# Moving the tile grid of a GELU-gated product by half a tile, with GELU in place

## The chip, the core and the metric

The kernel runs on one core of one Trainium2 chip. The metric is the device time in microseconds (us). Three runs of the kernel before gave 469.43, 469.44 and 469.3, so the median is 469.43 us.

The core has several engines that run at the same time. Three of them matter here: ScalarE (ACT in the profile) computes GELU, VectorE (DVE) multiplies, and SyncE (SP) only issues transfers. ScalarE issues transfers as well. A transfer issued from SP goes to one DMA queue (q1 in the profile), one issued from ScalarE to another (q10), and the same 16 DMA engines serve both queues. An instruction that has to wait for a semaphore holds up everything behind it on its own engine.

## The reference

```python
batch, seq, dim = (32, 512, 2048)          # float32
x1, x2 = x[..., :1024], x[..., 1024:]
gelu_x1 = 0.5 * x1 * (1 + erf(x1 / np.sqrt(2)))
return (gelu_x1 * x2).astype(np.float32)
```

Flattened, x is 16,384 rows of 2,048 numbers (134.2 MB), and the output is 16,384 rows of 1,024 numbers (67.1 MB).

## The kernel before

The rows are cut into 16 tiles. A tile has 128 partitions with R = 8 consecutive rows in each, so a partition of a tile is one run of 64 KB in x and one run of 32 KB in the output. A load of a tile moves 8.4 MB, a store 4.2 MB. There are two input buffers (x0_tile, x1_tile) and two output buffers (o0_tile, o1_tile); tile i uses number i % 2 of each.

The order of the work is written out by hand with semaphores; no scheduler changes it. For each tile i, in steps of some rows (5 and 3 for an ordinary tile; 2, 2 and 4 for the first and the last):

- ScalarE (line 87) reads the left half of the rows from the input buffer and writes GELU of it into the output buffer. Ahead of the first step it waits for `ready[k]`. This semaphore counts both the load of tile i and the store of tile i-2, so ScalarE starts a tile when its input has landed and the output buffer is free.
- VectorE (line 95) waits for that GELU and multiplies the output buffer in place by the right half of the input buffer.
- Behind the last step, SP waits for the products of tile i and issues the load of tile i+2 (line 115, the transfer itself on line 49), and ScalarE waits for the same products and issues the store of tile i (lines 112 and 56). The stores of the last two tiles are issued by SP.

The first tile is loaded in two halves of four rows, each with a semaphore of its own (`first`), and stored in two halves of four rows. The last tile is stored in two halves too. A small transfer into a scrap tile (line 63) opens ScalarE's queue at the start. At the end the semaphores are cleared, and SP waits for `tail_stored`, which counts the three stores that SP issued.

Of the kernel before, what the change touches and what calls it, by code (L numbers as in the profile page):

```python
# [1 line left out]

# [4 lines left out]

GELU = mybir.ActivationFunctionType.Gelu


@with_exitstack
def kernel(
    ctx: ExitStack,
    tc: tile.TileContext,
    x: bass.AP,
    out: bass.AP,
):
    nc = tc.nc
    P = nc.NUM_PARTITIONS

    x_flat = x.flatten_outer_dims()
    out_flat = out.flatten_outer_dims()
    n_rows, dim = x_flat.shape
    half = dim // 2

    R = 8
    x_t = x_flat.rearrange("(n p r) d -> n p r d", p=P, r=R)
    o_t = out_flat.rearrange("(n p r) d -> n p r d", p=P, r=R)
    n_tiles = x_t.shape[0]
    x_bufs = [nc.alloc_sbuf_tensor(f"x{k}_tile", [P, R, dim], x.dtype) for k in range(2)]  # L30
    o_bufs = [nc.alloc_sbuf_tensor(f"o{k}_tile", [P, R, half], out.dtype) for k in range(2)]

    first = [nc.alloc_semaphore(f"first{j}") for j in range(2)]
    ready = [nc.alloc_semaphore(f"ready{k}") for k in range(2)]
    gelu_done = nc.alloc_semaphore("gelu_done")
    mul_done = nc.alloc_semaphore("mul_done")
    tail_stored = nc.alloc_semaphore("tail_stored")
    opened = nc.alloc_semaphore("opened")  # L40
    scrap = nc.alloc_sbuf_tensor("scrap_tile", [8, 128], x.dtype)
    n = {sem.name: 0 for sem in [*first, *ready, gelu_done, mul_done, tail_stored, opened]}

    def counted(ins, sem, by):
        ins.then_inc(sem, by)
        n[sem.name] += by

    def load(i, rows, sem):
        ins = nc.sync.dma_start(out=x_bufs[i % 2][:, rows, :], in_=x_t[i][:, rows, :])  # L49
        counted(ins, sem, 16)  # L50
        return ins

    def store(queue, i, rows, sem):
        queue.wait_ge(mul_done, n[mul_done.name])
        counted(
            queue.dma_start(out=o_t[i][:, rows, :], in_=o_bufs[i % 2][:, rows, :]), sem, 16
        )

    opening = nc.scalar.dma_start(out=scrap[:, :], in_=x_t[0][:8, 0, :128])
    counted(opening, opened, 16)
    for ins in (
        opening,
        load(0, slice(0, 4), first[0]),
        load(0, slice(4, 8), first[1]),
        load(1, slice(0, 8), ready[1]),
    ):  # L70
        tc.no_tile_sem_insts.add(ins.ins.name)
    tc.close()
    tc.compile()  # L73

    for i in range(n_tiles):
        k = i % 2
        last = i == n_tiles - 1
        pieces = i == 0 or last
        steps = ((0, 2), (2, 4), (4, 8)) if pieces else ((0, 5), (5, 8))
        for lo, hi in steps:  # L80
            rows = slice(lo, hi)
            if i == 0 and lo % 4 == 0:
                nc.scalar.wait_ge(first[lo // 4], 16)
            elif lo == 0:
                nc.scalar.wait_ge(ready[k], n[ready[k].name])
            counted(
                nc.scalar.activation(  # L87
                    out=o_bufs[k][:, rows, :], in_=x_bufs[k][:, rows, :half], func=GELU
                ),
                gelu_done,  # L90
                1,
            )
            nc.vector.wait_ge(gelu_done, n[gelu_done.name])
            counted(
                nc.vector.tensor_mul(  # L95
                    out=o_bufs[k][:, rows, :],
                    in0=o_bufs[k][:, rows, :],
                    in1=x_bufs[k][:, rows, half:],
                ),
                mul_done,  # L100
                1,
            )
            if pieces and hi % 4 == 0:
                if last:
                    store(nc.sync, i, slice(hi - 4, hi), tail_stored)
                else:
                    store(nc.scalar, i, slice(hi - 4, hi), ready[k])
        if not pieces:
            if i == n_tiles - 2:
                store(nc.sync, i, slice(0, R), tail_stored)  # L110
            else:
                store(nc.scalar, i, slice(0, R), ready[k])
        if i + 2 < n_tiles:
            nc.sync.wait_ge(mul_done, n[mul_done.name])
            load(i + 2, slice(0, R), ready[k])


    nc.scalar.wait_ge(opened, 16)
    nc.scalar.drain()  # L119
    for sem in (*first, *ready, opened):  # L120
        nc.scalar.sem_clear(sem)
    nc.vector.drain()
    nc.vector.sem_clear(gelu_done)
    nc.sync.sem_clear(mul_done)
    nc.sync.wait_ge(tail_stored, n[tail_stored.name]).then_inc(
        tail_stored, -n[tail_stored.name]
    )


# [1 line left out]
_INS = ['x']  # L131
_OUTS = [((32, 512, 1024), 'float32')]


# [23 lines left out]
```

## Time and profile before

| what | value |
|---|---|
| runs | 469.43, 469.44, 469.3 us; median 469.43 us |
| span of the profiled execution, first to last instruction | 467.8 us |
| time outside the span, median less span | 1.6 us |
| VectorE busy | 140.5 us, 30% of the span, 34 products |
| ScalarE busy | 115.5 us, 25% of the span, 34 GELUs and a table load |
| moved by DMA | 201.34 MB, mean 430 GB/s |
| GELU of 5, 4, 3, 2 rows | 4.469, 3.608, 2.747, 1.901 us |
| product of 5, 4, 3, 2 rows | 5.493, 4.424, 3.351, 2.288 us |
| load of a full tile, issue to landing | median 44.4 us |
| store of a full tile from ScalarE, issue to landing | median 44.7 us |

The profiled execution gives its span; the time outside it, 1.6 us, is the difference from the median and is taken as the same for both kernels. A busy time is the time in which the engine worked. The DMA figures come from records of single packets; a packet here is one run of one partition, and one transfer of a 128-partition tile gives 8 packets to each of the 16 DMA engines. The shares of the queues are shares of the 16 engines' time together. Each transfer also has 16 packets of a few bytes, which signal its semaphore.

### The profile page before, as it was taken

How to read it: one execution, taken by the hardware profiler on the slowest of the kernel's cores; microseconds unless marked ns; L12 is line 12 of the kernel's file. 1: busy time of each engine (PE TensorE's matmuls, PEld its weight loads, DVE VectorE, ACT ScalarE, POOL GpSimd, SP SyncE). 2: the span in 40 equal slices, each digit the busy share in tenths (PEclk: the TensorE clock that was granted, in tenths of full speed). 3: DMA queues.
4: the chain of work that ended last, by engine and by line, in shares of the span. 5: the costliest groups of instructions: out<-in, count | busy, mean ns of one | idle time of the engine just before them, and what ended most of it. 6: DMA issues, size and time to landing. Idle time of an engine off the chain costs nothing.

```text
span 467.8 us, 154 instructions
## 1 busy us (share of the span) xinstructions
DVE 140.5 (30%) x34; ACT 115.5 (25%) x35; POOL 0.2 (0%) x4
## 2 busy tenths in 40 slices
DVE  0330515207051060511606115060150702507043
ACT  1320606041060410604105050050501506014060
POOL 0000000000000000000000000000000000000000
DMA  8999999999999999999999999999999999999988
GB/s 359 448 448 448 398 406 496 403 403 448 459 437 403 440 412 493 403 403 448 487 409 403 445 406 493 403 403 448 493 403 403 448 426 471 403 426 426 493 384 379
DMA packets 5057, 201.34 MB, mean 430 GB/s; under 512 B 568, under 2 KB 576, under 8 KB 576
## 3 DMA queue, kind: packets, MB, share of 16 engines
q1 hardware_dynamic: 2880, 142.61, 70.6%
q10 hardware_dynamic: 2176, 58.73, 29.1%
q14 instruction: 1, 0.01, 0.0%
HBM read 134.22 MB, written 67.11 MB: 430 GB/s over the span
## 4 chain that ended last, share of the span: by engine, by line
DMA 76%; DVE 14%; ACT 8%; ACTq 0%; SPq 0%; issue 0%
DMA out_dram<-o_tile 66%; DVE o_tile L95 14%; DMA x_tile<-in_x_dram 10%; ACT o_tile L87 8%; ACTq L119 0%; SPq L49 0%
## 5 line engine op out<-in xcount | busy, mean ns | idle before, releaser
L95 DVE TENSOR_TENSOR o_tile<-o_tile,x_tile 128x5120 f32<-128x5120 f32 (+3 forms) x34 | 140.5, 4171 | 319.7 <-ACT o_tile L87 319.7
L87 ACT ACTIVATE o_tile<-x_tile 128x5120 f32<-128x5120 f32 (+3 forms) x34 | 114.3, 3407 | 337.3 <-DMA out_dram<-o_tile 301.8
L87 ACT ACT_TABLE_LOAD x1 | 1.3, 1283 | 2.9 <-PEq L73 2.9
L142 POOL MEMSET const-bfloat16-1.0<- 128x1 bf16 x1 | 0.1, 102 | 0.0
L142 POOL MEMSET const-uint8-127<- 128x1 uint8 x1 | 0.1, 101 | 0.0
L142 POOL MEMSET const-float32-0.0<- 128x1 f32 x1 | 0.1, 99 | 0.2 <-issue 0.2
L142 POOL MEMSET const-float32-1.0<- 128x1 f32 x1 | 0.1, 98 | 0.0
## 6 DMA issues: line engine op xcount, KB each, us to landing
out_dram<-o_tile ACTq DMA_DIRECT2D x13, 4096.0 KB, 44.7
x_tile<-in_x_dram SPq DMA_DIRECT2D x2, 4096.0 KB, 16.7
out_dram<-o_tile ACTq DMA_DIRECT2D x2, 2048.0 KB, 34.4
out_dram<-o_tile SPq DMA_DIRECT2D x1, 4096.0 KB, 25.2
out_dram<-o_tile SPq DMA_DIRECT2D x2, 2048.0 KB, 7.8
x_tile<-in_x_dram SPq DMA_DIRECT2D x15, 44.4
scrap_tile<-in_x_dram ACTq DMA_DIRECT2D x1, 4.0 KB
```

Source lines behind the costliest of these rows:

```text
L87: nc.scalar.activation(out=o_bufs[k][:, rows, :], in_=x_bufs[k][:, rows, :half], func=GELU),
L95: nc.vector.tensor_mul(out=o_bufs[k][:, rows, :], in0=o_bufs[k][:, rows, :], in1=x_bufs[k][:, rows, half:],),
L142: nc = _bacc.Bacc("TRN2", target_bir_lowering=False, num_devices=1)
```

## The change

The grid of tiles is moved by half a tile. There are now 17 tiles: the first and the last have four rows a partition, the fifteen between have eight. The first tile is one load of four rows, and the second, of eight rows, is queued right behind it. The first tile is stored in two pieces of two rows; the last is stored whole.

GELU is written back over the left half of the input buffer, and the product goes from the input buffer to the output buffer. ScalarE therefore no longer waits for the store of tile i-2 ahead of GELU: the semaphore `ready` is split into `loaded`, for which ScalarE waits, and `stored`, for which VectorE waits ahead of the first product of a tile. The last tile's product is written into the input buffer of the tile before it, so that it waits for no store. The number of products and GELUs stays 34 each, the number of stores 18; the number of loads goes from 18 to 17.

```diff
-    R = 8
-    x_t = x_flat.rearrange("(n p r) d -> n p r d", p=P, r=R)
-    o_t = out_flat.rearrange("(n p r) d -> n p r d", p=P, r=R)
-    n_tiles = x_t.shape[0]
+    R, EDGE = 8, 4
+    bounds = [0, EDGE * P, *range((EDGE + R) * P, n_rows, R * P), n_rows]
+    n_tiles = len(bounds) - 1
+    depth = [(bounds[i + 1] - bounds[i]) // P for i in range(n_tiles)]
...
-    first = [nc.alloc_semaphore(f"first{j}") for j in range(2)]
-    ready = [nc.alloc_semaphore(f"ready{k}") for k in range(2)]
+    loaded = [nc.alloc_semaphore(f"loaded{k}") for k in range(2)]
+    stored = [nc.alloc_semaphore(f"stored{k}") for k in range(2)]
...
+    def out_tile(i):
+        if i == n_tiles - 1:
+            flat = x_bufs[(i - 1) % 2].rearrange("p r d -> p (r d)")
+            return flat[:, : R * half].rearrange("p (r d) -> p r d", r=R)
+        return o_bufs[i % 2]
...
-        pieces = i == 0 or last
-        steps = ((0, 2), (2, 4), (4, 8)) if pieces else ((0, 5), (5, 8))
+        steps = ((0, 2), (2, 4)) if depth[i] == EDGE else ((0, 5), (5, 8))
+        products_before = n[mul_done.name]
         for lo, hi in steps:
-            rows = slice(lo, hi)
-            if i == 0 and lo % 4 == 0:
-                nc.scalar.wait_ge(first[lo // 4], 16)
-            elif lo == 0:
-                nc.scalar.wait_ge(ready[k], n[ready[k].name])
-            counted(
-                nc.scalar.activation(
-                    out=o_bufs[k][:, rows, :], in_=x_bufs[k][:, rows, :half], func=GELU
-                ),
-                gelu_done,
-                1,
-            )
+            if lo == 0:
+                nc.scalar.wait_ge(loaded[k], n[loaded[k].name])
+            gelu = x_bufs[k][:, lo:hi, :half]
+            counted(nc.scalar.activation(out=gelu, in_=gelu, func=GELU), gelu_done, 1)
             nc.vector.wait_ge(gelu_done, n[gelu_done.name])
+            if lo == 0 and last:
+                nc.vector.wait_ge(mul_done, products_before)
+            elif lo == 0 and n[stored[k].name]:
+                nc.vector.wait_ge(stored[k], n[stored[k].name])
             counted(
                 nc.vector.tensor_mul(
-                    out=o_bufs[k][:, rows, :],
-                    in0=o_bufs[k][:, rows, :],
-                    in1=x_bufs[k][:, rows, half:],
+                    out=out_tile(i)[:, lo:hi, :], in0=gelu, in1=x_bufs[k][:, lo:hi, half:]
                 ),
                 mul_done,
                 1,
             )
-            if pieces and hi % 4 == 0:
-                if last:
-                    store(nc.sync, i, slice(hi - 4, hi), tail_stored)
-                else:
-                    store(nc.scalar, i, slice(hi - 4, hi), ready[k])
-        if not pieces:
-            if i == n_tiles - 2:
-                store(nc.sync, i, slice(0, R), tail_stored)
-            else:
-                store(nc.scalar, i, slice(0, R), ready[k])
+            if i == 0:
+                store(nc.scalar, i, lo, hi, stored[k])
         if i + 2 < n_tiles:
             nc.sync.wait_ge(mul_done, n[mul_done.name])
-            load(i + 2, slice(0, R), ready[k])
+            load(i + 2)
+        if i >= n_tiles - 2:
+            store(nc.sync, i, 0, depth[i], tail_stored)
+        elif i > 0:
+            store(nc.scalar, i, 0, R, tail_stored if i == n_tiles - 3 else stored[k])
```

More of the change, by code (lines that the diff above doesn't have):

```diff
@@ L24, with tile_of @@
     half = dim // 2
-    R = 8
-    x_t = x_flat.rearrange("(n p r) d -> n p r d", p=P, r=R)
-    o_t = out_flat.rearrange("(n p r) d -> n p r d", p=P, r=R)
-    n_tiles = x_t.shape[0]
+    R, EDGE = 8, 4
+    bounds = [0, EDGE * P, *range((EDGE + R) * P, n_rows, R * P), n_rows]
+    n_tiles = len(bounds) - 1
+    depth = [(bounds[i + 1] - bounds[i]) // P for i in range(n_tiles)]
+    def tile_of(flat, i):
+        return flat[bounds[i] : bounds[i + 1], :].rearrange("(p r) d -> p r d", p=P)
     x_bufs = [nc.alloc_sbuf_tensor(f"x{k}_tile", [P, R, dim], x.dtype) for k in range(2)]
     o_bufs = [nc.alloc_sbuf_tensor(f"o{k}_tile", [P, R, half], out.dtype) for k in range(2)]
-    first = [nc.alloc_semaphore(f"first{j}") for j in range(2)]
-    ready = [nc.alloc_semaphore(f"ready{k}") for k in range(2)]
+    loaded = [nc.alloc_semaphore(f"loaded{k}") for k in range(2)]
+    stored = [nc.alloc_semaphore(f"stored{k}") for k in range(2)]
     gelu_done = nc.alloc_semaphore("gelu_done")
@@ L41 @@
     scrap = nc.alloc_sbuf_tensor("scrap_tile", [8, 128], x.dtype)
-    n = {sem.name: 0 for sem in [*first, *ready, gelu_done, mul_done, tail_stored, opened]}
+    n = {
+        sem.name: 0
+        for sem in [*loaded, *stored, gelu_done, mul_done, tail_stored, opened]
+    }
     def counted(ins, sem, by):
@@ L46, in counted, with load, store @@
         n[sem.name] += by
-    def load(i, rows, sem):
-        ins = nc.sync.dma_start(out=x_bufs[i % 2][:, rows, :], in_=x_t[i][:, rows, :])
-        counted(ins, sem, 16)
+    def out_tile(i):
[3 more added lines that the diff above has]
+        return o_bufs[i % 2]
+    def load(i):
+        ins = nc.sync.dma_start(out=x_bufs[i % 2][:, : depth[i], :], in_=tile_of(x_flat, i))
+        counted(ins, loaded[i % 2], 16)
         return ins
-    def store(queue, i, rows, sem):
+    def store(queue, i, lo, hi, sem):
         queue.wait_ge(mul_done, n[mul_done.name])
         counted(
-            queue.dma_start(out=o_t[i][:, rows, :], in_=o_bufs[i % 2][:, rows, :]), sem, 16
+            queue.dma_start(out=tile_of(out_flat, i)[:, lo:hi, :], in_=out_tile(i)[:, lo:hi, :]),
+            sem,
+            16,
         )
-    opening = nc.scalar.dma_start(out=scrap[:, :], in_=x_t[0][:8, 0, :128])
+    opening = nc.scalar.dma_start(out=scrap[:, :], in_=x_flat[:8, :128])
     counted(opening, opened, 16)
[L65 to L70, printed above, removed]
+    for ins in (opening, load(0), load(1)):
         tc.no_tile_sem_insts.add(ins.ins.name)
@@ L102 @@
             )
-            if pieces and hi % 4 == 0:
-                if last:
-                    store(nc.sync, i, slice(hi - 4, hi), tail_stored)
-                else:
-                    store(nc.scalar, i, slice(hi - 4, hi), ready[k])
-        if not pieces:
-            if i == n_tiles - 2:
-                store(nc.sync, i, slice(0, R), tail_stored)
-            else:
-                store(nc.scalar, i, slice(0, R), ready[k])
+            if i == 0:
+                store(nc.scalar, i, lo, hi, stored[k])
         if i + 2 < n_tiles:
             nc.sync.wait_ge(mul_done, n[mul_done.name])
-            load(i + 2, slice(0, R), ready[k])
+            load(i + 2)
[3 more added lines that the diff above has]
+            store(nc.scalar, i, 0, R, tail_stored if i == n_tiles - 3 else stored[k])
     nc.scalar.wait_ge(opened, 16)
     nc.scalar.drain()
-    for sem in (*first, *ready, opened):
+    nc.scalar.sem_clear(opened)
+    for sem in loaded:
         nc.scalar.sem_clear(sem)
     nc.vector.drain()
-    nc.vector.sem_clear(gelu_done)
+    for sem in (gelu_done, *stored):
+        nc.vector.sem_clear(sem)
     nc.sync.sem_clear(mul_done)
```

## The prediction

> **What bounds the kernel now.** I read the page first. Both compute engines are idle for most of the span, and the row of the DMA engines is full.
>
> ```profile
> span 467.8 us, 154 instructions
> DVE 140.5 (30%) x34; ACT 115.5 (25%) x35; POOL 0.2 (0%) x4
> q1 hardware_dynamic: 2880, 142.61, 70.6%
> q10 hardware_dynamic: 2176, 58.73, 29.1%
> DMA 76%; DVE 14%; ACT 8%; ACTq 0%; SPq 0%; issue 0%
> ```
>
> The queue shares add up to 99.7% of 16 engines' span. The fifth line, the chain that ended last, puts 22% on DVE and ACT, which suggests exposed compute; so I ask the waits next.
>
> ```profile
> ACT o_tile L87 <- DMA out_dram<-o_tile: 301.8, 14, 21.9
> ```
>
> ScalarE waited 301.8 us for stores in 14 waits. That is the wait the change takes from it. Whether it cost time depends on what the DMA engines did meanwhile, so the third view is the table by windows (length, DVE, ACT, POOL, clock, DMA share, GB/s):
>
> ```profile
> 1.70:467.40 465.70, 140.48 (x34) 115.54 (x35) 0.00 (x0) 1.00 1.00 432
> 129.40:419.40 290.00, 87.61 (x20) 71.23 (x20) 0.00 (x0) 1.00 1.00 434
> ```
>
> From 1.7 to 467.4 us the 16 DMA engines are busy at share 1.00, and over ten tiles in the middle they move 434 GB/s. While one tile is computed, the transfers of the other fill the engines. The chain follows waits, but the time is set by bytes: all 201 MB go through engines that never pause.
>
> Last I read the DMA view in three windows: ten middle tiles (129.4 to 419.4), 30 to 42, and 460.2 to 461.2 (packets, MB, share):
>
> ```profile
> q1 hardware_dynamic: 1440, 83.89, 66.7%
> q10 hardware_dynamic: 1440, 41.94, 33.5%
> ...
> q1 hardware_dynamic: 64, 4.19, 81.4%
> q10 hardware_dynamic: 64, 1.05, 20.4%
> ...
> q14 instruction: 1, 0.01, 1.9%
> ```
>
> They show two things. The queues alternate packet by packet, 64 against 64, even where a store packet (16 KB) is a quarter of a load packet (64 KB). And they price packets. In the first window each queue has 1280 data packets and 160 signals: a load packet takes 66.7% x 16 x 290 / 1280 = 2.418 us, a 32 KB store packet 33.5% gives 1.214. In the second, 16 KB takes 20.4% x 16 x 12 / 64 = 0.612. In the third, one 8 KB packet (of instructions) takes 1.9% x 16 x 1 = 0.304. Time goes with bytes.
>
> **The change, part by part.** *Packets.* Full loads stay 15 and half loads 2. Full stores go from 14 to 15, 16 KB stores from 4 to 1, and two 8 KB stores are new. A transfer is 8 packets an engine, so an engine's load work stays 120 x 2.418 + 16 x 1.213 = 309.6 us, and its store work goes from 112 x 1.213 + 32 x 0.612 = 155.4 to 120 x 1.213 + 8 x 0.612 + 16 x 0.304 = 155.3. The total is 465.0 before and 464.9 after: -0.1 us. The 8 KB price is the one unknown: no store packet of that size is in the trace. Bounds are half of 16 KB (0.304 agrees) and no saving at all against 16 KB (0.612), so 0 to +4.9 us; I take the lower, as 64, 32 and 16 KB are proportional within 1.5%.
>
> *The load removed.* One DMA issue fewer (0.42 us on SP at 1.16 in the chain, ahead of nothing but load 1): nothing. The first packet waits for the first issue, at 0.73, as before.
>
> *Start.* Load 0 lands as before, and GELU starts at 12.79. On ScalarE the first store now stands between the two GELUs and waits for the first product, so the sequence is 1.90 + 2.29, a store at about 17.0, 0.36 of issue, 1.90 + 2.29, a store at 21.6. SP issues load 2 then, not at 30.6. Queue q1 still has load 1 (8 x 2.418 = 19 us from about 11.1), so the engines are covered. Store packets begin after some 12 load packets (8 of load 0, 4 of load 1), at 20.8: an estimate from the first store before, which was issued at 19.26 and still had no packet in the window 20.5 to 24.2, so 1.0 us (first issue to first packet at 0.73 to 1.7) to 5.2 us of lag.
>
> *Middle.* From there one load packet goes with one store packet. Tile 0's stores are 16 small packets an engine, not 8, so the stores run 8 packets more behind the loads: load i (1 to 15) ends at load packet 8 + 8i, store i at store packet 16 + 8i, that is at load packet 28 + 8i. The product of tile i waits for store i-2 (load packet 12 + 8i), four packets after load i has ended. Then it takes 5.49 + 3.35 = 8.84, and load i+2 is issued. Load i+1 has four packets left at the wait's end, 4 x (2.418 + 1.213) = 14.5 us, against 0.4 (landing: last packet at 467.4, span's end at 467.8) + 8.84 + 1.0 to 5.2 = 10.2 to 14.4. So q1 just does not run dry. If it does, q10 still holds a whole store and the engines go on. Behind VectorE's waiting product nothing else stands; behind its result stand SP's load and ScalarE's store, and behind that store the next GELU. So ScalarE still stops at store i-2, by way of the product. In the trace this costs nothing while a queue holds packets; without that cover a period would show its 13.3 us of compute, 4.47 + 8.84.
>
> *GELU in place, other addresses, three semaphore clears more on VectorE's and ScalarE's queues*: the same row counts at the same prices on engines 70% and 75% idle; the clears run under the last stores. Nothing.
>
> *End.* Store 13 ends at load packet 132, four into load 16's eight. From that point E the queues hold 4 load and 8 store packets of 32 KB, 12 x 1.213 = 14.6 us. Store 15's first packet comes 10.2 to 14.4 after E: no gap. Load 16 has landed by E + 10.1, GELU and product of 2 + 2 rows end by E + 16.7, and store 16 is queued there, while stores 14 and 15 hold the engines until 14.6 + 8 x 1.213 = 24.3. Then 8 x 0.612, and the end at E + 29.2, with no pause in the engines. The end before is as tight: share 0.94 in its last 7.2 us, so about 0.3 us is to be had.
>
> Sum: 467.8 - 0.1 for packets, 0 to -0.3 at the end, 0 elsewhere. I take 467.8, and with 1.6 outside the span 469.4 us.
>
> **Rivals.** *Faster: a fixed cost of each transfer is on the path, and one load fewer saves it.* For it: one issue disappears, and a store's wait leaves ScalarE. Against it: the engines are busy from 1.7 to 467.4, so all that is not packets is 1.7 + 0.4 + (465.7 - 465.0) = 2.8 us, and the first packet's 1.7 and the landing's 0.4 stay. The most that it could give is 0.7, or 468.7. To pass 0.2% (0.94 us, about what a measurement here can tell from no change) it needs faster packets too: about 468.3. Chance 0.04.
> The Trainium skill, "DMA: Bandwidth & Descriptors", section "Anatomy of one DMA", charges each DMA some 2.0 us of setup and completion besides its bytes; a load fewer would then be an estimated 2.0 us, 467.4. The trace disagrees for queued transfers: 434 GB/s across twenty of them leaves no room for it.
>
> *Slower: the small stores cost by the packet.* If an 8 KB packet takes what 16 KB takes, 16 x (0.612 - 0.304) = 4.9 us come on top: 474.3. It decides from 0.304 + 0.94 / 16 = 0.36 us a packet on. For it: no 8 KB store has run here. Against: the 0.304 row and the proportion. Chance 0.04.
> The Trainium skill, "DMA: Bandwidth & Descriptors", section "Bandwidth", gives 6.15 us for 1 MB (measured there on transfers issued from GpSimd); tile 0's stores are just that size, and at 2.42 us by this trace's 434 GB/s each would lose an estimated 3.7 us, 476.9 for two. In the window 30 to 42, with small stores beside a load, the trace shows 437 GB/s together, which speaks against it.
>
> *Slower: a gap at the end.* If store packets begin one load packet later, or a store lands more slowly than 0.4, the cover after E is 13.3 instead of 14.6 against up to 14.4, and both queues are empty for up to 1.1 us: 470.5. It decides from 14.6 us between E and store 15's first packet. For it: store 15 comes from a product that now waits for a store. Against: the lag must be at its upper bound. Chance 0.07.
>
> *The wait only changes its owner.* ScalarE stops at its own store instruction, which waits for the product, which waits for the older store. I hold this to be so in the middle, and it gives the same time as the forecast, 469.4.
>
> **Numbers.** The forecast holds with 0.85: engines full before and after, the same bytes. Faster 0.04, slower 0.04 + 0.07 = 0.11. The range goes from 469.0, the 0.3 at the end and 0.1 for packets, to 470.3, most of the gap.
>
> **What would show it.** Right: DMA share 1.00 from 1.7 to the end, 434 GB/s in the middle, first stores landing near 62 us, ScalarE's waits for stores gone from the list and about as long on loads, VectorE waiting for stores. The 8 KB stores' packets should have a share that gives 0.30 us each. Wrong: a window with a share below 0.9, above all between 440 and 460, or a load packet longer than 2.42 beside 8 KB ones.

## The result and the profile after

The changed kernel takes 470.08 us (median of 19 runs) where the kernel before takes 469.30 (19 runs). The ratio is 1.0017 with a 95% interval of 1.0010 to 1.0023. So it is slower by 0.8 us: less than the 0.94 us that the prediction took for the limit of what can be told from no change, but the interval of these runs does not hold 1. The direction "no change" was wrong, by a small amount.

The page of the changed kernel, its busy times, queues and chain:

```profile
span 468.2 us, 169 instructions
DVE 140.5 (30%) x34; ACT 115.6 (25%) x35; POOL 0.2 (0%) x4
q1 hardware_dynamic: 2736, 140.51, 69.6%
q10 hardware_dynamic: 2320, 60.82, 30.1%
DMA 81%; DVE 15%; ACT 1%; DVEq 1%; issue 0%; ACTq 0%
```

Its list of waits (who waited for what: us in total, times, longest):

```profile
ACT x_tile L88 <- DMA x_tile<-in_x_dram: 332.8, 17, 22.1
DVE o_tile L95 <- DMA out_dram<-o_tile: 276.8, 14, 20.7
```

The change did what it says. ScalarE's 301.8 us of waits for stores are gone; it waits 332.8 us for loads, and VectorE has the 276.8 us of waits for stores. The chain that ended last now has 1% of ScalarE in place of 8%.

The table by windows (length, DVE, ACT, POOL, clock, DMA share, GB/s) shows the DMA engines as full as before:

```profile
1.70:467.40 465.70, 140.48 (x34) 115.64 (x35) 0.00 (x0) 1.00 1.00 432
129.40:419.40 290.00, 87.61 (x21) 71.22 (x20) 0.00 (x0) 1.00 1.00 434
```

The middle moves the same 434 GB/s. The 0.8 us are therefore neither in the middle nor in idle DMA engines. Two places remain: the time outside the span, and transfers that run but take too long.

**Outside the span.** Every run has its time and its span. In 35 runs of the kernel before, the median span is 468.0 and the time outside 1.33 us; in the changed kernel's 19 runs they are 468.5 and 1.62. So 0.3 us of the 0.8 lie outside the span and 0.5 inside. (The execution that the prediction used, 467.8, was one of the shortest of the kernel before; hence its 1.6 outside.) The changed execution of the page, 468.2, is one of the shortest of its 19 too.

**Inside the span.** The DMA view by windows prices single load packets: the window holds the start of one packet on each of the 16 engines, so share x window x 16 / packets is the mean time of one. At 60.4 to 61.4, and at 62.9 to 63.9 (packets, MB, share):

```profile
q1 hardware_dynamic: 16, 1.05, 241.8%
q10 hardware_dynamic: 16, 0.13, 30.9%
...
q1 hardware_dynamic: 16, 1.05, 294.8%
q10 hardware_dynamic: 16, 0.00, 0.9%
```

In the first window a 64 KB load packet takes 2.418 us, its usual time, and an 8 KB store packet 0.309. In the second, 2.5 us later, the same kind of load packet takes 2.948 us on all 16 engines. In it q10 has only the 16 signals of tile 0's second store: this is the load packet between the last 8 KB store packet and the first 32 KB one. A smaller one is at 30.1 to 30.8 (2.50 us), in the middle of tile 0's first store.

The kernel before has such a place as well, from 21.6 to 22.2, ahead of its first store packet at 24.4. The view counts 16 signals of 0.009 us with the 16 load packets, so a load packet there takes 445.6% x 16 x 0.6 / 16 less 0.009, or 2.66 us:

```profile
q1 hardware_dynamic: 32, 1.05, 445.6%
```

I went through the packet records of each trace in this way: for every data packet, its time less the usual one for its size (2.418, 1.213, 0.611 or 0.309 us), summed from 12 to 100 us and divided by 16 engines. The kernel before has 0.41 us of such excess, the changed kernel 0.68. After 100 us both have 0.02 or 0.03. Ahead of 12 us, where the first load packets run, the two pages have 0.60 and 0.76.

### The profile page after: what moved, and what is told of

It is laid out like the page before. It is cut to its first block, busy times and chain, and to the rows that moved or that the text cites. A ratio compares the mean times of both kernels' runs of the same rounds, so it can differ in the third digit from the quotient of the medians.

```text
span 468.2 us, 169 instructions
## 1 busy us (share of the span) xinstructions
DVE 140.5 (30%) x34; ACT 115.6 (25%) x35; POOL 0.2 (0%) x4
## 3 DMA queue, kind: packets, MB, share of 16 engines
q10 hardware_dynamic: 2320, 60.82, 30.1%
## 4 chain that ended last, share of the span: by engine, by line
DMA 81%; DVE 15%; ACT 1%; DVEq 1%; issue 0%; ACTq 0%
DMA out_dram<-o_tile 72%; DVE o_tile L95 14%; DMA x_tile<-in_x_dram 9%; ACT x_tile L88 1%; DVE x_tile L95 0%; DVEq L116 0%; ACTq L67 0%; DVEq L93 0%
## 5 line engine op out<-in xcount | busy, mean ns | idle before, releaser
L95 DVE TENSOR_TENSOR o_tile<-x_tile 128x5120 f32<-128x5120 f32 (+2 forms) x32 | 136.0, 4288 | 310.6 <-DMA out_dram<-o_tile 276.8
L88 ACT ACTIVATE x_tile<-x_tile 128x5120 f32<-128x5120 f32 (+2 forms) x34 | 114.4, 3407 | 335.6 <-DMA x_tile<-in_x_dram 332.8
L95 DVE TENSOR_TENSOR x_tile<-x_tile 128x2048 f32<-128x2048 f32 x2 | 4.5, 2288 | 5.3 <-ACT x_tile L88 5.3
```

The costliest lines, as they stand in the source:

```text
L88: counted(nc.scalar.activation(out=gelu, in_=gelu, func=GELU), gelu_done, 1)
L95: nc.vector.tensor_mul(out=out_tile(i)[:, lo:hi, :], in0=gelu, in1=x_bufs[k][:, lo:hi, half:]),
```

## The experiments

Times and ratios are against the kernel before on the same chip, whose median was 469.24 to 469.32 us in every group.

### Once more, as a yardstick, and three parts of the change

I began with three theories: A, the 8 KB stores and the long load packets behind them at 63 us; B, the moved waits and GELU in place; C, the end of the moved grid.

> The changed kernel once more, as the yardstick of this group and for a second trace. All theories: 469.9 to 470.3 us, ratio 1.0015 to 1.0020 to the kernel before. Theory A (the long load packets around 63 us, where ScalarE's queue goes over from 8 KB to 32 KB store packets, are the cost): they are there again, 16 of them, 0.4 us or more too long each. Theory B (waits) and theory C (the end) need no long packets at 63 us; if they are gone here and the time is still 470, theory A is wrong.

Measured: 470.17 us, ratio 1.0018 (1.0010 to 1.0027), span 468.5, outside 1.62. The excess was 0.76 us, at the same places (30, 52 and 63 us), but spread otherwise: 0.30 at 30 us and only 0.14 at 63. So theory A's "0.4 us each at 63 us" was too narrow; the sum repeats, the places share it differently.

Tile 0 stored whole:

```diff
-            if i == 0:
-                store(nc.scalar, i, lo, hi, stored[k])
...
-        elif i > 0:
-            store(nc.scalar, i, 0, R, tail_stored if i == n_tiles - 3 else stored[k])
+        else:
+            store(nc.scalar, i, 0, depth[i], tail_stored if i == n_tiles - 3 else stored[k])
```

> The changed kernel, but tile 0 is stored whole, with 16 KB packets, behind its second product; everything else as changed. Theory A: the 8 KB packets and the long load packets at 63 us go, 469.3 to 469.5. Theory B (VectorE's wait, GELU in place) and theory C (the end of the grid: a queue for each of the last two stores): 470.1 as changed.

Measured: 469.97 us, ratio 1.0019 (1.0011 to 1.0027). Theory A falls: without any 8 KB packet the time stays. The excess stays too, 0.78 us, now mostly in one load packet an engine at 31 us.

The grid alone:

```diff
-            gelu = x_bufs[k][:, lo:hi, :half]
-            counted(nc.scalar.activation(out=gelu, in_=gelu, func=GELU), gelu_done, 1)
+                if not last and n[stored[k].name]:
+                    nc.scalar.wait_ge(stored[k], n[stored[k].name])
+            raw = x_bufs[k][:, lo:hi, :half]
+            gelu = raw if last else out_tile(i)[:, lo:hi, :]
+            counted(nc.scalar.activation(out=gelu, in_=raw, func=GELU), gelu_done, 1)
...
-            elif lo == 0 and n[stored[k].name]:
-                nc.vector.wait_ge(stored[k], n[stored[k].name])
...
```

> The grid alone: 17 tiles and the stores of the changed kernel, but GELU goes to the output buffer and ScalarE waits for both the load and the store, as before; only the last tile is done in place. Theory A and theory C: 470.1 as changed. Theory B: back to 469.3.

Measured: 470.38 us, ratio 1.0022 (1.0014 to 1.0031), but made up differently: span 469.1, outside 1.31. The long packets at the start are there (0.80 us). Another 0.6 us comes at the end: here SP's queue had run empty before store 15 was issued at 451.8, and the first packets of that store, which start while ScalarE's queue still runs store 14, took up to 1 us too long. The DMA view from 452.6 to 453.6 shows it, 15 packets of 32 KB at 171.4% x 16 / 15 = 1.83 us, not 1.21:

```profile
q1 hardware_dynamic: 15, 0.49, 171.4%
```

The waits alone:

```diff
-                    out=o_bufs[k][:, rows, :], in_=x_bufs[k][:, rows, :half], func=GELU
+                    out=x_bufs[k][:, rows, :half], in_=x_bufs[k][:, rows, :half], func=GELU
...
             nc.vector.wait_ge(gelu_done, n[gelu_done.name])
+            if lo == 0 and n[stored[k].name]:
+                nc.vector.wait_ge(stored[k], n[stored[k].name])
...
-                    in0=o_bufs[k][:, rows, :],
+                    in0=x_bufs[k][:, rows, :half],
...
```

> The waits alone: 16 tiles, loads and stores of the kernel before, but GELU in place in the input buffer and VectorE waiting for stores. Theory A and theory C: 469.3 as before. Theory B: 470.1.

Measured: 469.59 us, ratio 1.0004 (0.9996 to 1.0013), span 468.1, outside 1.48. The interval holds 1, so the total decides little. What is plain is that the span hardly moves, while the time outside grows by 0.15.

These four split the question. The span's 0.5 us goes with the grid, the time outside with the waits and what was moved with them (1.31 where ScalarE waits for stores, 1.5 to 1.6 where VectorE does).

### The time outside the span

The semaphores that count stores are cleared at the end by the engine that waits for them. In the changed kernel VectorE clears three, before it cleared one. Here SP clears the two:

```diff
-    for sem in (gelu_done, *stored):
-        nc.vector.sem_clear(sem)
-    nc.sync.sem_clear(mul_done)
+    nc.vector.sem_clear(gelu_done)
+    for sem in (mul_done, *stored):
+        nc.sync.sem_clear(sem)
```

> The changed kernel, but the two semaphores that count stores are cleared by SP at the end, not by VectorE; VectorE clears one semaphore as before. So far the time outside the span is 1.3 us in the three kernels in which ScalarE waits for stores and 1.5 to 1.6 us in those in which VectorE waits. If VectorE's two added clears cost this: 1.3 outside, 469.8 in all. If it is VectorE's added waits (17 more instructions in its program) or anything else: 1.6 outside, 470.1. The span stays at 468.5 by all theories.

Measured: 469.73 us, ratio 1.0012 (1.0003 to 1.0021), span 468.4, outside 1.34 (1.31 to 1.37 in 11 runs). The 0.28 us are gone. They came from VectorE's two added clears, although in the trace these end at 456.6, some 12 us before the span does. VectorE's added waits, which are all still there, cost nothing outside. Nor do the two clears on ScalarE, where the kernel with the grid alone has them (1.31). The price is not a fixed one: the kernel with the waits alone has the same two clears more on VectorE, and there the time outside grew by 0.15.

Taking the last clear from VectorE in the kernel before as well would then make that kernel faster, if the price were per clear:

```diff
-    nc.vector.sem_clear(gelu_done)
-    nc.sync.sem_clear(mul_done)
+    for sem in (mul_done, gelu_done):
+        nc.sync.sem_clear(sem)
```

> The kernel before, but the one semaphore that VectorE clears at the end is cleared by SP too. If each clear on VectorE costs 0.14 us outside the span (0.28 for two), the time outside falls from 1.33 to 1.2 and the time to 469.15. If only more than one clear costs, nothing changes: 469.3.

Measured: 469.19 us, ratio 1.0000 (0.9991 to 1.0009), outside 1.32. It is no price per clear: the first costs nothing. What takes the time outside the span was not seen, as no record lies there.

### The start or the end of the grid

Theory A had failed, and of theory B only the time outside was left, which came from the clears. For the span I put three others: S, load packets of 64 KB that run from 12 us on beside the first stores; E, the end of the grid; R, a queue that is slow when it is used first.

Tile 1 loaded in two halves, so that the order of loads at the start is nearer to that before (the deciding line):

```diff
...
+        pieces = ((0, 4), (4, 8)) if i == 1 else ((0, depth[i]),)
...
```

> The changed kernel, but tile 1 is loaded in two halves of four rows (32 KB packets), so that 64 KB packets begin after the third half load and not after the first. Theory S (start: in the changed grid the first stores and the first refill run beside 64 KB load packets from 12 us on, and some of these take up to 0.6 us too long): 469.5 or less, and the long packets between 20 and 70 us add up to 0.4 us an engine or less, not 0.7. Theory E (end of the grid): 470.1 as changed. Theory R (a queue's descriptors are slow the first time): 470.1, long packets at other places.

Measured: 470.17 us, ratio 1.0016 (1.0006 to 1.0027). Theory S in that form falls: it is not the 64 KB load packets, since here 32 KB load packets at 19 to 22 us are too long, 0.47 us an engine, and the excess from 12 to 100 us is 0.8 as in the changed kernel. (The traced run was the longest of the 11, 471.63 us: one engine ended 1.8 us behind the mean of the 16, and its span is no measure here.)

The moved end on the start of before (fifteen tiles of eight rows, then two of four; tile 0 loaded and stored in halves):

```diff
-    bounds = [0, EDGE * P, *range((EDGE + R) * P, n_rows, R * P), n_rows]
+    bounds = [*range(0, n_rows, R * P), n_rows - EDGE * P, n_rows]
...
```

> The start of the kernel before (tile 0 of eight rows, loaded and stored in halves) with the waits, the in-place GELU and the end of the changed kernel (two tiles of four rows at the end, the last product in an input buffer). Theory S: 469.4 to 469.6, as the waits alone gave. Theory E: 470.1.

Measured: 472.75 us, ratio 1.0078 (1.0065 to 1.0090), which neither theory had. The windows view of its end says why:

```profile
450.00:458.60 8.60, 0.00 (x0) 0.01 (x1) 0.00 (x0) 1.00 0.99 425
458.60:465.00 6.40, 4.47 (x2) 3.70 (x2) 0.00 (x0) 1.00 0.58 250
```

The last load lands at 458.6, level with the last full store; GELU and product of the last tile then run beside one half store alone, which lands at 463.4; the queues are empty until the last store is issued at 465.1, and the engines' share falls to 0.58. This is the gap of the prediction's rival, in a neighbour of the change. It says nothing on theory E, because the changed kernel has no such gap (share 1.00 up to 467.4). Against theory E stands the changed kernel's own trace, whose packets after 100 us are too long by 0.02 us an engine in all. The start of this run has the 0.4 us of excess of the kernel before, with the changed waits, so the excess goes with the start; its span, with the gap in it, decides nothing.

### Small packets in a queue

Three more small transfers at the start:

```diff
...
+    for j in range(3):
+        ins = nc.scalar.dma_start(out=warm_tile[:, j, :], in_=x_flat[:128, j * 128 : j * 128 + 128])
+        counted(ins, opened, 16)
...
```

> The changed kernel with three more small transfers (128 partitions x 512 bytes each into a scrap tile) at the start on ScalarE's queue, so that all 16 engines have used that queue before the first store. Their own cost is 24 packets an engine of 0.025 us each, 0.6 us. Theory R: the long load packets beside the first stores go (-0.7), so the time stays at 470.0 or falls. Theories S and E: 470.1 + 0.6 = 470.7.

Measured: 473.52 us, ratio 1.0090 (1.0076 to 1.0104). Theory R is not tested by the time, as the small transfers did something else. The DMA view of this kernel from 17 to 23 us:

```profile
q1 hardware_dynamic: 48, 3.15, 122.7%
q10 hardware_dynamic: 48, 0.02, 1.1%
```

48 packets of 0.02 MB in all (32 of 512 bytes and 16 signals) take turns with 48 load packets of 64 KB. A packet of 512 bytes costs 0.025 us but has to wait a whole load packet for its turn, so 24 of them an engine put tile 0's first store back, from a landing at 42.0 us to one at 75.2. The products that wait for it come late, and the queues run empty near 87 us.

The kernel before with 8 KB stores for the first half of tile 0:

```diff
-            if pieces and hi % 4 == 0:
+            if i == 0 and hi <= 4:
+                store(nc.scalar, i, slice(lo, hi), ready[k])
+            elif pieces and hi % 4 == 0:
```

> The kernel before, but the first half of tile 0 is stored in two pieces of two rows (8 KB packets). Theories S and E: 469.3 to 469.5. If small store packets themselves cost, against the run with one store for tile 0: 469.6 to 470.0.

Measured: 474.22 us, ratio 1.0125 (1.0104 to 1.0145; two of its five runs are near 476.5). The same again: three stores of 8 packets an engine, one more than before, make the last of tile 0's stores land at 88.6 us, not at 71.4. ScalarE waits for it ahead of tile 2. The load and the store that follow tile 2's products are issued at 101.9, after the load queue has run dry at 93.5 and store 1 has landed at 100.8. Its windows:

```profile
90.00:100.00 10.00, 6.87 (x2) 5.75 (x2) 0.00 (x0) 1.00 0.93 400
100.00:107.00 7.00, 2.06 (x2) 4.67 (x2) 0.00 (x0) 1.00 0.68 211
```

The miss is mine: I had looked at the price of the packets and not at the number of turns. The changed kernel has 16 packets an engine for tile 0's stores, this one 24, and here ScalarE still needs 13.3 us behind a store, not 8.8.

### How the stores begin

This leaves theory F: the load packets that run while the stores begin take too long, and the way in which the stores begin sets how long.

The changed kernel without tile 0's stores:

```diff
-            if i == 0:
-                store(nc.scalar, i, lo, hi, stored[k])
```

> The changed kernel without the two stores of tile 0 (those output rows are left out; 2.1 MB, 4.8 us less). Only the trace matters. If the long load packets around 30 us come from the loads alone (the load after the first two on that queue), they are there at the same place, 0.1 to 0.6 us each. If they come from stores beside loads, nothing is long before the first store of tile 1 is under way (about 45 us); then some are long there, about 0.25 us.

The trace has no long load packet at all between 12 and 48 us, where loads run alone. The one ahead of the first store packet, from 48.2 to 48.9, is then the longest of all, 515.2% x 16 x 0.7 / 16 = 3.61 us in place of 2.42:

```profile
q1 hardware_dynamic: 16, 1.05, 515.2%
```

So the excess comes with the beginning of stores beside loads, and here, where the stores begin with 32 KB packets at once, it is 1.2 us, five times what was expected for this case.

Two earlier kernels, whose queues had run empty, fit this where loads and stores start anew together. In the kernel before with 8 KB stores, from 102.8 to 103.4 us, a load packet takes 633.3% x 16 x 0.6 / 16 = 3.80 us, and the next store packet comes at 106.6:

```profile
q1 hardware_dynamic: 16, 1.05, 633.3%
```

In the kernel with three small transfers it is 3.90 us at 87.4 to 88.0. In both it is also the first load packet behind a pause, so they alone would not decide. Theory R, a queue that is slow when it is used first, does not explain every long packet: the one at 63 us in the changed kernel comes when all 16 engines have used both queues for 40 us.

If the beginning of the stores is the cause, the kernel before, with its old grid, can be made to pay it by storing tile 0 whole:

```diff
-            if pieces and hi % 4 == 0:
+            if i == 0:
+                if hi == R:
+                    store(nc.scalar, i, slice(0, R), ready[k])
+            elif pieces and hi % 4 == 0:
```

> The kernel before, but tile 0 is stored whole behind its last product, as one store of 32 KB packets; the grid, the waits and the end are as before. Theory F (the load packets that run while the first stores begin are the too long ones, and how the stores begin sets how long): as in the run without tile 0's stores, a load packet of 3.6 us in place of 2.42 stands ahead of the first 32 KB store packet at about 35 us; long packets sum to 1.2 us an engine instead of 0.4, and the time is 469.8 to 470.2. If the long packets belong to the moved grid: none above 0.3 us, 469.2 to 469.4.

Measured: 469.81 us (median of 11), ratio 1.0021 (1.0012 to 1.0031; four of its runs are near 471, and the medians alone give 1.0011), span 468.5, outside 1.33. From 33.8 to 34.3 us, ahead of the first store packet, the load packets take 685.0% x 16 x 0.5 / 16 = 3.43 us:

```profile
q1 hardware_dynamic: 16, 1.05, 685.0%
```

No other packet between 12 and 100 us is too long, and the excess is 1.0 us. The old grid, the old waits and the old end, with only the first store changed, give the span of the changed kernel. So a start of stores can cost this much; the reverse, the new grid with a start that costs less, was not run.

Three more traces of the kernel before:

> The kernel before once more, for a second trace. Theory S: its load packets between 20 and 70 us are too long by 0.35 to 0.5 us an engine in sum, against 0.68 to 0.79 in the three traces of the changed grid. If the sum is 0.6 or more here, the long packets don't explain the difference of the spans.

> The kernel before, a third trace. Theory F: the time of the run goes with its long packets: about 0.4 us an engine between 20 and 80 us in a run of 469.3, 0.7 in one of 469.6.

> The kernel before, a fourth trace, as the third: 0.4 us an engine between 20 and 80 us at 469.3, 0.7 at 469.6.

| kernel | time of the traced run | span | excess 12 to 100 us |
|---|---|---|---|
| before, page shown | not known | 467.8 | 0.41 |
| before, third | 469.22 | 467.9 | 0.44 |
| before, fourth | 469.31 | 468.0 | 0.54 |
| before, second | 469.66 | 468.3 | 0.69 |
| before, no clear on VectorE | 469.32 | 468.0 | 0.57 |
| before, waits alone changed | 469.80 | 468.3 | 0.57 |
| changed | 469.56 | 468.2 | 0.68 |
| changed, once more | 469.81 | 468.3 | 0.76 |
| changed, two clears on SP | 469.62 | 468.3 | 0.70 |
| changed, tile 0 stored whole | 470.04 | 468.3 | 0.78 |
| before, tile 0 stored whole | 469.78 | 468.4 | 1.01 |

Among the four traces of the kernel before, the span goes with the excess, as theory F has it. The second has the long load packet at 70.4 us, between the last 16 KB and the first 32 KB store packet (449.5% x 16 x 0.6 / 16 gives 2.70 us a load packet; the window from 70.4 to 71), which the first doesn't have. This packet lies outside the window that was named beforehand: from 20 to 70 us the second trace has only 0.41 us, and the fit depends on the wider window. The third and fourth traces met runs of 469.2 and 469.3 (0.43 and 0.54 us from 20 to 80), so no other run near 469.6 was traced.

Span and excess are not tied closely: the last two traces on the old grid both have 0.57 us, with spans of 468.0 and 468.3. The excess is a mean over the 16 engines, and the span ends with the slowest of them. That one ends 0.3 us behind the mean in the first of the two and 0.6 in the second. A better measure is therefore the mean end of the 16 engines' last signals: 467.23 us over the four traces of the kernel before (467.11 to 467.40), 467.52 over the first three of the changed kernel in the table (467.50 to 467.53), 467.74 for the kernel before with tile 0 stored whole.

Of the 35 runs of the kernel before, five had a span of 468.2 or more, of the changed kernel's 19 all. What those five met, no trace shows.

## Why the prediction was right or wrong

*The middle* was right. The engines are as full, the rate is 434 GB/s in both kernels, and moving the wait from ScalarE to VectorE gave nothing, because the engines had no pause to lose. ScalarE does stop at its own store instruction, as predicted, but not for longest: it issues store 14 at 421.26, as the product ends, and then waits for load 15 until 430.53.

*Packets* was right in the price of the one unknown (0.304 predicted, 0.309 measured) and wrong in taking the price of a load packet as constant, 2.418 us for all 120. That is the first step that failed: some load packets that run while the stores begin take 2.5 to 3.6 us. The prediction had itself named a load packet longer than 2.42 as a sign of being wrong. In the traces, this term is 0.52 us for the kernel before and 0.71 for the changed one, means over the four and the three traces named above. That gives 0.2 of the 0.3 us by which the mean end of the engines moved. The other 0.1 is already there when load 0 ends (its signals come at 12.21 and 12.31 us on average), although the prediction had it land as before; the reason is open.

So 0.3 us of the span's 0.5 are accounted for. The other 0.2 are in runs without a trace: the three traced runs of the changed kernel have spans of 468.2 and 468.3, its median run 468.5. That the way in which the stores begin sets the excess is shown for the old grid, by the run with tile 0 stored whole. For the moved grid it is inferred from that run. The places fit it in part: in the changed kernel the load packets at 63 us stand ahead of the first 32 KB store packets, but those at 30 us stand in the middle of a store, and what makes them long stays open.

*The semaphore clears* were put at nothing, under the last stores. They do lie there in the trace, and yet VectorE's two more cost 0.28 us outside the span. The prediction took the time outside as the same for both kernels; that was the second step that failed, and it is the one that an experiment settles, since moving two clears to SP brought the time outside back from 1.62 to 1.34. It also counted them loosely: VectorE has two more, ScalarE two fewer.

*Start* and *Middle* had the times nearly right (stores at 17.2 and 21.9, tile 0's stores landed at 42.0 and 63.8, against about 62; load 2 issued at 21.9) with one thing left out: the signal of a transfer takes a turn too. A transfer is 9 turns and not 8, in both queues, so the order of loads and stores came out as predicted. Behind the last 8 KB store packets, at 60.4, the signals had to wait for one more load packet, so the first 32 KB store packet came at 66.1 us.

*End* was right: no gap, the last store was issued 7.0 us before the store ahead of it landed (456.4 and 463.4). Load 16 landed 2.0 us later than the sum had it (at 449.9, and store 13 at 437.8), which cost nothing. The rival of a gap did not happen, but a neighbour of the change, the moved end on the old start, fell into it and was 3.5 us slower. The rival of the small packets was wrong in its form: an 8 KB packet doesn't cost what a 16 KB one costs. But the two runs with more small packets were 4 to 5 us slower than the kernel before, by the turns that these packets took.

*Faster by one transfer less* did not happen. The Trainium skill's fixed 2.0 us for each DMA ("DMA: Bandwidth & Descriptors", section "Anatomy of one DMA") would have shown as 2.0 us less, and the time rose. That section gives the figure for transfers issued from GpSimd, and those of this kernel are issued from SP and ScalarE; the prediction did not say so.

## What to carry to other kernels

When all DMA engines are busy from first to last, a change of waits or of buffers that opens no gap moved the time here only by about a microsecond or less (the three runs that opened one were 3.5 to 5 us slower), so look at what is not in the sum: the few transfers at the beginning of a new stream, and the time outside the span. Count the turns of a queue, not only its bytes: where two queues alternate, as here, a small packet delays everything behind it in its own queue by one packet of the other. And leave the clearing of semaphores to an engine on which it costs nothing, which a run of its own has to tell.

## What was not expected of the hardware

- While stores begin beside loads, some load packets take longer: 64 KB in 2.50 to 3.61 us in place of 2.42 within the first 75 us, often just ahead of the first store packets or of the first larger ones. Where both queues began together behind a pause, it was 3.80 and 3.90 us. Where a store began on SP's queue beside another store, its 32 KB packets took 1.83 us in place of 1.21. With 32 KB stores from the start it was one packet an engine and 1.0 to 1.2 us; with smaller ones first it was spread over two or three places, and 0.4 to 0.95 us. Why a beginning stream does this, and why the places share the sum differently from run to run, stays open.
- Two added semaphore clears on VectorE, 12 us ahead of the end, cost 0.28 us outside the span (0.15 in the kernel with the waits alone); on SP they cost nothing, and a first one on VectorE costs nothing either. What they delay stays open.
- Two queues alternate by packets whatever their size: 48 packets of 512 bytes and signals against 48 of 64 KB.
